# Weight splits off POOL, rope tables queued late, convolution banks copied out raw, and a first stage fed by quarters of x

## The chip, the cores and the metric

The kernel runs on one core of a Trainium2 chip. It holds one program with five engines: TensorE (PE, with PEld for its weight loads), VectorE (DVE), ScalarE (ACT), GpSimd (POOL) and SyncE (SP). PE multiplies into PSUM, DVE and ACT do elementwise work, POOL does a little of it, SP issues most transfers. The time is the device time of one launch in microseconds. Three runs of the kernel before took 995.56, 997.72 and 1001.56 us, the median is 997.72 us.

## The reference

Two decoder layers over 256 tokens of width 1024. Each layer is a half-weighted SwiGLU feed-forward stage (FFN), a mixer, and another FFN; in layer 0 the mixer is a gated short convolution beside cross-attention over 256 memory tokens, in layer 1 it is causal attention on a shared compressed key/value (MLA) beside the same cross-attention. Everything is float32.

```python
def swiglu(h, w13, w2):
    gate, up = jnp.split(h @ w13, 2, axis=-1)
    return (jax.nn.silu(gate) * up) @ w2

def short_conv_mixer(h, w_in, conv_w):
    proj = h @ w_in
    gate_b, gate_c, xt, q_mem = jnp.split(proj, [CONV_CH, 2 * CONV_CH, 3 * CONV_CH], axis=-1)
    return gate_b * causal_short_conv(gate_c * xt, conv_w), q_mem

for layer in range(2):
    x = x + 0.5 * swiglu(rms_norm(x, g[layer, 0]), w13[layer, 0], w2[layer, 0])
    h = rms_norm(x, g[layer, 1])
    ...                                   # mixer: convolution (0) or MLA (1), and memory attention
    x = x + jnp.concatenate([y_mix, y_mem], -1) @ w_out[layer]
    x = x + 0.5 * swiglu(rms_norm(x, g[layer, 2]), w13[layer, 1], w2[layer, 1])
```

D_MODEL is 1024 and D_FF 2816. rms_norm divides each token by the root of its mean square.

## The kernel before, in words

The residual stream `xT` stays in SBUF, channels on partitions, as 8 blocks of 128 channels by 256 tokens. Weights stream from HBM in units of 128 x 1024 (512 KB).

**Splits.** PE multiplies in a reduced-precision float32 mode, so each operand is split into a high part (a rounded cast on ACT) and a low part (raw minus high, a two-input subtraction). A product is then three matmuls (`mm3`), or, where the moving side holds high and low next to each other in 512 columns, a 512-column one and a 256-column one (`mm2`, L193 and L194); below this couple is called a pair. The low part of a weight unit is L87, run on DVE, or on POOL for the units named in `on_pool`: column block 2 of each FFN (two units) and the first w2 unit of each FFN, and three units of the convolution's input weights (`CIN_POOL`).

**Streams.** Class `Stream` A carries w13, the mixers' input weights and the memory weights, B carries w2 and the output weights. Each loads some units ahead (SP issues), casts them (ACT, L86) and subtracts (L87), in the order in which they will be used. A has four raw buffers and six split ones, B two and four.

**An FFN** (`ffn`) has 22 column blocks j. Block j takes two A units (the lower and the upper half of x's channels, c = 0 and 1), 8 pairs each, into two PSUM banks (`pg`, `pm`). ACT copies half a bank out, DVE adds the other half (L434, L435), DVE multiplies by the row factor R (L439), then SiLU (ACT), gate times up (DVE), a split of that product, and 24 matmuls with w2 that accumulate in four banks `acc`.

**The row factor.** The norm's 1/rms per token isn't applied to x. Projections of raw x start at once, and R scales them afterwards. `r_row` makes it: PE sums squares over channels (L289, called r_col below), DVE takes a reciprocal root in a chain of some twelve tiny 128x2 instructions (L165, L153 to L160), DVE builds two diagonal matrices `dg` (L301), PE spreads them (L303), DVE copies R (L306).

**The mixer of layer 0** (`conv_mixer`) takes 20 A units in ten blocks (n = 0 to 9), 24 matmuls a unit, into one bank each; the bank pool `pg` has two banks. Its blocks are read out of PSUM by DVE with R at once (L648), so the first two banks come free only after R, and R's matmul stands ahead of the last quarter of the first two blocks (`pairs`, `late` false).

**The start.** SP issues x in four quarters and the first A units in pieces (unit 0 in four, units 1 to 4 in two), in one queue; the gains of the norm come first. Unit by unit, blocks 0 and 1 are multiplied against the lower half of x, then against the upper half. The rope tables (cosine and sine of positions, about ten small DVE instructions and two on ACT, L704 to L729) stand in the FFN's block 3.

The code is recorded by a tile framework, which orders each engine's queue by its own list scheduling and adds semaphores; an engine then runs its queue strictly in that order.

Of the kernel before, what the change touches and what calls it, by code (L numbers as in the profile page):

```python
# [16 lines left out]
P = 128  # L17
T = 256
# [9 lines left out]
CIN_POOL = ((2, 0), (2, 1), (3, 1))  # L28
# [18 lines left out]
class Stream:  # L47


    def __init__(self, tc, raw_pool, hl_pool, name, units, load_ahead, split_ahead, pieces={}, on_pool=()):  # L50
# [5 lines left out]
        self.pieces, self.on_pool = pieces, on_pool  # L56
        self.hl = {}
        self.hold = ()

    def ahead(self, upto_load, upto_split):  # L60
        nc = self.tc.nc
        while self.loaded < min(upto_load, len(self.units)):
            key, src, n, own = self.units[self.loaded]
            r = self.raw_pool.tile([P, U], F32, name=f"{self.name}raw")
            pieces = self.pieces.get(self.loaded, 1)
            m = n // pieces
            for o in range(0, n, m):
                nc.sync.dma_start(out=r[:, o:o + m], in_=src[:, o:o + m])
            self.raw[self.loaded] = (r, pieces)
            self.loaded += 1  # L70
        while self.splitted < min(upto_split, self.loaded):
            key, src, n, own = self.units[self.splitted]
            r, pieces = self.raw.pop(self.splitted)
            self.split(r, pieces, n, own, nc.gpsimd if key in self.on_pool else nc.vector)
            self.splitted += 1

    def split(self, r, pieces, n, own, eng):
        nc = self.tc.nc
        h = None
        if own is not None:  # L80
            own(r)
        else:
            h = self.hl_pool.tile([P, 2, U], F32R, name=f"{self.name}hl")
            m = n // pieces
            for o in range(0, n, m):
                nc.scalar.copy(out=h[:, 0, o:o + m], in_=r[:, o:o + m])  # L86
                eng.tensor_tensor(out=h[:, 1, o:o + m], in0=r[:, o:o + m], in1=h[:, 0, o:o + m].bitcast(F32),  # L87
                                  op=ALU.subtract)
        self.hl[self.splitted] = h
# [17 lines left out]
def trunk(ctx: ExitStack, tc: tile.TileContext, a, out):  # L107
# [138 lines left out]
    for l in range(2):  # L246
# [144 lines left out]
    def pairs(keyf, row, bank=bank1):  # L391

        st = {}
        late = bank is not bank1

        def go(n):
            if n == 0:
# [8 lines left out]
            if n == 1:  # L406
                if late:
                    proj(keyf(1, 1), st["p1"], 1)
# [11 lines left out]
    def ffn(l, f, inserts, next_norm):  # L420
        go, st = pairs(lambda j, c: ("w13", l, f, j, c), r_row(xs["tot"], abank), lambda: (bank(), mbank()))
        ready = {}
        with tc.issue_after(xs["fed"][0].ins):
            A.ahead(A.used + 6, A.used + 6)
            B.ahead(B.used + 2, B.used + 1)

# [11 lines left out]
        def make(j, e):  # L438
# [8 lines left out]
            act = nc.scalar.activation(out=sl, in_=e[:, 0, :], func=AF.Silu)  # L447
            if j == 0:
# [180 lines left out]
    def conv_mixer(next_norm, pl):  # L629
# [4 lines left out]
        go, st = pairs(lambda j, c: ("cin", j, c), r_row(xs["tot"]))  # L634
# [7 lines left out]
        def project(upto):  # L642
            while st["n"] < upto:
# [3 lines left out]
                e = ev.tile([P, 2, T], F32, name="ev") if n else area[:, 0]  # L647
                evac = nc.vector.tensor_tensor(out=e, in0=ps, in1=rb(st["R"]), op=ALU.mult)  # L648
                if n == 0:
# [432 lines left out]
    for q in (1, 2, 3):  # L1082
        load_x(q)
# [124 lines left out]
```

## Time and profile before

| what | value |
|---|---|
| median of three runs | 997.72 us |
| the profiled execution | 996.72 us, its span 994.9 us |
| mean granted clock of TensorE | 0.995 of full speed |
| PE / DVE / ACT / POOL busy | 98% / 74% / 55% / 7% of the span |
| HBM traffic | 174 GB/s over the span |

The span runs from the first to the last instruction, some 1.8 us lie around it. Busy shares are of the whole span; the stages differ, so the rows further down are taken from single stretches. Times in rows are microseconds from the span's start. In a timeline row the first number is the start, the second the duration; square brackets hold the engine's idle time before it and what ended it. PEclk is the granted clock of TensorE as a share of 2.4 GHz: 0.50 is the lower level, 1.2 GHz.

### The profile page before, as it was taken

Reading aid. Unit: us, or ns where it says so; the run is one execution under the profiler, and the core shown is the slowest. Engines: PE = TensorE matmul, PEld = TensorE weight load, DVE = VectorE, ACT = ScalarE, POOL = GpSimd, SP = SyncE. Lnnn points to the kernel's source line nnn. Section 1 sums busy time; section 2 is a strip of 40 time slices with the busy share of each in tenths; the row PEclk is TensorE's granted clock in tenths of the full one; section 3 lists DMA queues with packets and bytes.
Section 4 is the critical chain, followed back from the end, with each engine's and each line's share of the span. In section 5 each row is a group of like instructions: output and inputs, shape, how many; then the busy total and the mean of one; then the engine's idle time right before and its main releaser. Section 6 shows DMA issues by size and latency. Waiting matters only on the chain.

```text
span 994.9 us, 16997 instructions
## 1 busy us (share of the span) xinstructions
PE 971.8 (98%) x6602; PEld 893.3 (90%) x6602; DVE 734.8 (74%) x1325; ACT 551.0 (55%) x933; POOL 67.6 (7%) x73
## 2 busy tenths in 40 slices
PE   7899999998999999999999999999999999999998
PEld 6789999998989999999999998899997999999997
DVE  6998666676876787666669887766689789666653
ACT  5666545555453655555547555555556776555541
POOL 4120000002001200000011100000011020000000
PEclk9999999999999999999999999999999999999999
DMA  7677656651655286665535765556324428655611
GB/s 265 222 251 241 194 187 190 183 178 64 209 160 171 62 296 210 188 188 186 179 101 180 233 209 185 179 185 188 114 97 127 149 85 312 189 182 186 187 47 43
DMA packets 50192, 174.18 MB, mean 175 GB/s; under 512 B 5824, under 2 KB 6848, under 8 KB 50112
## 3 DMA queue, kind: packets, MB, share of 16 engines
q1 hardware_dynamic: 49968, 172.98, 54.3%
q8 instruction: 51, 0.84, 0.3%
q14 instruction: 29, 0.24, 0.1%
q10 hardware_dynamic: 144, 0.13, 0.0%
HBM read 172.04 MB, written 1.05 MB: 174 GB/s over the span
## 4 chain that ended last, share of the span: by engine, by line
PE 87%; DVE 7%; DMA 2%; ACT 1%; issue 1%; SPq 0%; DVEq 0%; ACTq 0%
PE pm L193 16%; PE pg L193 15%; PE acc L187 10%; PE acc L188 10%; PE acc L189 10%; PE pm L194 8%; PE pg L194 8%; PE pg L187 2%; PE pg L188 2%; PE pg L189 2%; DVE ahl L87 1%; DMA braw<-in_wo 1%; PE pm L187 1%; PE pm L189 1%; PE pm L188 1%
## 5 line engine op out<-in xcount | busy, mean ns | idle before, releaser
L87 DVE TENSOR_TENSOR ahl<-araw,ahl 128x1024 fp32r<-128x1024 f32 (+3 forms) x216 | 254.0, 1180 | 84.8 <-ACT ahl L86 84.4
L86 ACT CAST ahl<-araw 128x1024 fp32r<-128x1024 f32 (+4 forms) x228 | 229.8, 1012 | 128.1 <-PE pm L194 83.0
L193 PE MATMUL pg<-xs,ahl 128*128 128x512 f32 x704 | 258.3, 400 | 3.5 <-DVE xs L183 3.1
L193 PE MATMUL pm<-xs,ahl 128*128 128x512 f32 x704 | 257.5, 400 | 0.7 <-DVE rsy_kn L160 0.7
L188 PE MATMUL acc<-g,bhl 128*128 128x256 f32 x832 | 235.8, 284 | 0.0
L189 PE MATMUL acc<-g,bhl 128*128 128x256 f32 x832 | 235.0, 283 | 0.0
L187 PE MATMUL acc<-g,bhl 128*128 128x256 f32 x832 | 233.7, 284 | 0.6 <-ACT g L179 0.6
L194 PE MATMUL pg<-xs,ahl 128*128 128x256 f32 x704 | 198.6, 282 | 0.1
L194 PE MATMUL pm<-xs,ahl 128*128 128x256 f32 x704 | 197.9, 281 | 0.0
L87 DVE TENSOR_TENSOR bhl<-braw,bhl 128x1024 fp32r<-128x1024 f32 x100 | 122.3, 1224 | 60.1 <-ACT bhl L86 59.7
L193 PEld LDWEIGHTS pg<-xs,ahl 128*128 128x128 f32 x704 | 133.2, 189 | 32.8 <-DVE xs L183 3.8
L193 PEld LDWEIGHTS pm<-xs,ahl 128*128 128x128 f32 x704 | 132.5, 188 | 33.5 <-issue 1.0
L187 PEld LDWEIGHTS acc<-g,bhl 128*128 128x128 f32 x832 | 157.3, 190 | 5.7 <-ACT g L179 1.4
L188 PEld LDWEIGHTS acc<-g,bhl 128*128 128x128 f32 x832 | 158.5, 191 | 0.3 <-DVE g L180 0.2
L189 PEld LDWEIGHTS acc<-g,bhl 128*128 128x128 f32 x832 | 158.6, 191 | 0.1
L86 ACT CAST bhl<-braw 128x1024 fp32r<-128x1024 f32 x104 | 108.7, 1048 | 79.2 <-PE acc L189 53.7
L194 PEld LDWEIGHTS pg<-xs,ahl 128*128 128x128 f32 x704 | 134.0, 190 | 1.3 <-DVE ahl L87 1.3
L194 PEld LDWEIGHTS pm<-xs,ahl 128*128 128x128 f32 x704 | 133.3, 189 | 0.1
L434 ACT COPY sq<-pm 128x256 f32<-128x256 f32 x88 | 32.8, 373 | 69.6 <-PE pm L194 69.3
L439 DVE TENSOR_TENSOR ev<-ev,R 128x512 f32<-128x512 f32 x88 | 61.5, 702 | 2.3
L435 DVE TENSOR_TENSOR ev<-pm,sq 128x256 f32<-128x256 f32 x88 | 37.1, 421 | 32.8 <-ACT sq L434 32.6
L447 ACT ACTIVATE silu<-ev 128x256 f32<-128x256 f32 x88 | 36.6, 417 | 36.7 <-DVE ev L439 36.6
(319 smaller groups left out, 1133.5 us busy)
## 6 DMA issues: line engine op xcount, KB each, us to landing
araw<-in_w SPq DMA_DIRECT2D x171, 512.0 KB, 3.7
braw<-in_w SPq DMA_DIRECT2D x88, 512.0 KB, 4.2
araw<-in_cin SPq DMA_DIRECT2D x20, 512.0 KB, 3.6
braw<-in_wo SPq DMA_DIRECT2D x16, 512.0 KB, 3.8
araw<-in_wmem SPq DMA_DIRECT2D x8, 512.0 KB, 4.3
araw<-in_qin SPq DMA_DIRECT2D x5, 512.0 KB, 3.5
araw<-in_w SPq DMA_DIRECT2D x8, 256.0 KB, 5.5
araw<-in_mem SPq DMA_DIRECT2D x4, 512.0 KB, 4.7
```

The source lines that it names most:

```text
L86: nc.scalar.copy(out=h[:, 0, o:o + m], in_=r[:, o:o + m])
L87: eng.tensor_tensor(out=h[:, 1, o:o + m], in0=r[:, o:o + m], in1=h[:, 0, o:o + m].bitcast(F32), op=ALU.subtract)
L187: nc.tensor.matmul(o, lhs[0], rhs[0], start=start, stop=False, skip_group_check=True)
L188: nc.tensor.matmul(o, lhs[0], rhs[1], start=False, stop=False, skip_group_check=True)
L189: nc.tensor.matmul(o, lhs[1], rhs[0], start=False, stop=stop, skip_group_check=True)
L193: nc.tensor.matmul(o, lhs[0], x, start=start, stop=False, skip_group_check=True)
L194: nc.tensor.matmul(o[:, 0, :], lhs[1], x[:, 0, :], start=False, stop=stop, skip_group_check=True)
L434: nc.scalar.copy(out=part[:, s, :], in_=ps[s][:, 1, :])
L435: nc.vector.tensor_tensor(out=e[:, s, :], in0=ps[s][:, 0, :], in1=part[:, s, :], op=ALU.add)
L439: evac = nc.vector.tensor_tensor(out=e, in0=e, in1=rb(st["R"]), op=ALU.mult)
L447: act = nc.scalar.activation(out=sl, in_=e[:, 0, :], func=AF.Silu)
```

## The change

1. `on_pool` and `pieces` go. Every weight unit's low part is made on DVE.
2. The rope tables move from block 3 to block 15 of the first FFN, and wait for the block before to be evacuated.
3. In `conv_mixer` R is taken after all of blocks 0 and 1. Their two banks are copied out raw by ACT and multiplied by R afterwards in SBUF (`arrived` holds what followed an evacuation before).
4. The first FFN has a head of its own: x in quarters q, and of the first four units the halves that belong to quarter q. After each quarter come 8 pairs: blocks 0 and 1, two channel blocks. The transfers are issued from two queues: SP has all of x, the later units and the rest, ACT has the gains and three pieces of units 0 and 1. The units after that are loaded and split as the quarters pass.

```diff
-    A = Stream(tc, araw, ahl, "a", a_units, 6, 5, {0: 4, 1: 2, 2: 2, 3: 2, 4: 2},
-               {("w13", l, f, 2, c) for l in range(2) for f in range(2) for c in range(2)}
-               | {("cin", j, c) for j, c in CIN_POOL})
-    pool_split = {("w2", l, f, j) for l in range(2) for f in range(2) for j in (0,)}
-    B = Stream(tc, braw, bhl, "b", b_units, 3, 2, {}, pool_split)
+    A = Stream(tc, araw, ahl, "a", a_units, 6, 5)
+    B = Stream(tc, braw, bhl, "b", b_units, 3, 2)
...
+            if n == 0 and head is not None:
+                st["p0"], st["p1"] = bank(), bank()
+                for q in range(4):
+                    head(q)
+                    c = q // 2
+                    for j in range(2):
+                        ps = st[f"p{j}"]
+                        w = heads[2 * c + j]
+                        for k in (2 * q, 2 * q + 1):
+                            for s in range(2):
+                                o = k % 4 * 256 + s * P
+                                mm2(ps[s], (w[:, 0, o:o + P], w[:, 1, o:o + P]), xs["hl"][:, k], k == 0, k == KD - 1)
+                        if q == 3 and j == 0:
+                            next(row)
...
-        go, st = pairs(lambda j, c: ("cin", j, c), r_row(xs["tot"]))
+        go, st = pairs(lambda j, c: ("cin", j, c), r_row(xs["tot"]), late=True)
...
+            if st["n"] == 0:
+                es = [area[:, 0], ev.tile([P, 2, T], F32, name="ev")]
+                for n, e in enumerate(es):
+                    nc.scalar.copy(out=e, in_=go(n))
+                for n, e in enumerate(es):
+                    evac = nc.vector.tensor_tensor(out=e, in0=e, in1=rb(st["R"]), op=ALU.mult)
+                    arrived(n, e, evac)
+                st["n"] = 2
...
+    nc.scalar.dma_start(out=gc[:, 0:8], in_=a["cols"][:, 0:8])
+    load_x(nc.sync, 0)
+    load_w(nc.scalar, 0, 0, 256)
+    load_w(nc.sync, 0, 256, 256)
+    load_w(nc.scalar, 1, 0, 512)
+    load_x(nc.sync, 1)
+    load_w(nc.scalar, 0, 512, 512)
+    load_w(nc.sync, 1, 512, 512)
+    load_x(nc.sync, 2)
+    load_w(nc.sync, 2, 0, 512)
+    load_w(nc.sync, 3, 0, 512)
+    load_x(nc.sync, 3)
+    load_w(nc.sync, 2, 512, 512)
+    load_w(nc.sync, 3, 512, 512)
     nc.sync.dma_start(out=gc[:, 8:], in_=a["cols"][:, 8:])
+    nc.sync.dma_start(out=pos_i, in_=a["pos"])
...
+    def first_head(q):
+        c, o = q // 2, q % 2 * 512
+        feed_split(q, 0)
+        for i in (2 * c, 2 * c + 1):
+            for p in (0, 256) if q == 0 and i == 0 else (0,):
+                n = 256 if q == 0 and i == 0 else 512
+                A.split(raws[i], heads[i], o + p, n)
         feed_square(q, q < 2)
-    A.ahead(5, 4)
-    nc.sync.dma_start(out=pos_i, in_=a["pos"])
+        if q == 2:
+            A.ahead(HEAD + 2, HEAD)
+        if q == 3:
+            B.ahead(1, 0)
+            A.ahead(HEAD + 4, HEAD + 2)
 
     def rope_later():
-        rope_tables(w1)
+        with tc.issue_after(xs["evac"]), tc.issue_after(xs["act"]):
+            rope_tables(w1)
         yield
```

What this does to the queues is shown at three places. First PE in the first stage, where R's matmul (reading `dg`) stands. Banks 232 and 233 are those of column block 1 before, 374 that of block 2; in the changed kernel 368 and 369 are those of block 2. Before:

```order
L194 MATMUL pm_233<-xs_123,ahl_207 128x256
L193 MATMUL pm_233<-xs_123,ahl_207 128x512
L194 MATMUL pm_233<-xs_123,ahl_207 128x256
L193 MATMUL pg_374<-xs_123,ahl_215 128x512
L303 MATMUL acc3_323<-dg_322,ones_108 128x128 x2
L194 MATMUL pg_374<-xs_123,ahl_215 128x256
```

Now (the line of R's matmul is L300):

```order
L194 MATMUL pm_369<-xs_122,ahl_269 128x256
L193 MATMUL pm_369<-xs_122,ahl_269 128x512
L194 MATMUL pm_369<-xs_122,ahl_269 128x256
L193 MATMUL pg_368<-xs_122,ahl_272 128x512
L300 MATMUL acc3_316<-dg_315,ones_108 128x128 x2
L194 MATMUL pg_368<-xs_122,ahl_272 128x256
```

Before, R's matmul follows the 32 pairs of blocks 0 and 1; now it follows those and the 8 pairs of block 2's first unit. Between r_col and R's matmul stand 13.5 pairs before and 12 now.

Then DVE in the first stage, in the middle of the root's chain. Before:

```order
L155 TENSOR_SCALAR rsy_x<-rsy_x 128x2
L704 CAST pos_f<-pos_i 128x2
L158 SCALAR_TENSOR_TENSOR rst_x<-rsy_x 128x2
L707 TENSOR_SCALAR r_ang<-gc,pos_f 128x32
L159 TENSOR_TENSOR rst_x<-rst_x,var_x 128x2
L707 TENSOR_SCALAR r_ang<-gc,pos_f 128x32
L160 SCALAR_TENSOR_TENSOR rsy_x<-rst_x,rsy_x 128x2
L435 TENSOR_TENSOR ev<-pm,sq 128x256
```

Now (L452 is the evacuation that was L435):

```order
L155 TENSOR_SCALAR rsy_x<-rsy_x 128x2
L452 TENSOR_TENSOR ev<-pg,sq 128x256
L158 SCALAR_TENSOR_TENSOR rst_x<-rsy_x 128x2
L452 TENSOR_TENSOR ev<-pm,sq 128x256
L159 TENSOR_TENSOR rst_x<-rst_x,var_x 128x2
L559 TENSOR_TENSOR mem_gqk<-gc 128x1
L844 TENSOR_TENSOR mla_gqk<-gc 128x1
L160 SCALAR_TENSOR_TENSOR rsy_x<-rst_x,rsy_x 128x2
```

The rope tables' instructions have left the chain; the four evacuations of blocks 0 and 1 stand in it.

Last DVE in the convolution, from the middle of the same chain to the first weight splits. Before:

```order
L160 SCALAR_TENSOR_TENSOR rsy_x<-rst_x,rsy_x 128x2
L301 TENSOR_SCALAR dg<-ident,rsy_x 128x128 x2
L306 COPY R<-pm 128x256
L648 TENSOR_TENSOR spare<-pg,R 128x512
L648 TENSOR_TENSOR ev<-pg,R 128x512
L87 TENSOR_TENSOR ahl<-araw,ahl 128x1024 x2
L87 TENSOR_TENSOR bhl<-braw,bhl 128x1024 x2
```

Now (weight splits are L68, and the two multiplications by R, L666, read SBUF):

```order
L160 SCALAR_TENSOR_TENSOR rsy_x<-rst_x,rsy_x 128x2
L68 TENSOR_TENSOR ahl<-araw,ahl 128x1024
L158 SCALAR_TENSOR_TENSOR rst_x<-rsy_x 128x2
L159 TENSOR_TENSOR rst_x<-rst_x,var_x 128x2
L160 SCALAR_TENSOR_TENSOR rsy_x<-rst_x,rsy_x 128x2
L158 SCALAR_TENSOR_TENSOR rst_x<-rsy_x 128x2
L159 TENSOR_TENSOR rst_x<-rst_x,var_x 128x2
L160 SCALAR_TENSOR_TENSOR rsy_x<-rst_x,rsy_x 128x2
L298 TENSOR_SCALAR dg<-ident,rsy_x 128x128 x2
L303 COPY R<-pm 128x256
L666 TENSOR_TENSOR spare<-spare,R 128x512
L666 TENSOR_TENSOR ev<-ev,R 128x512
```

One weight split that POOL made now stands inside the chain, and two more follow it, where before only those of DVE's own units did. At the other three FFN starts one A and one B unit now stand ahead of the chain's first instruction.

## Rows read from the trace of the kernel before

**Rows 1.** What PE waited for, whole span: total us, times, longest us.
```profile
PE acc L303 <- DVE dg L301: 5.8, 1, 5.8
PE pg L193 <- DVE xs L183: 3.1, 2, 2.6
PE pm L303 <- DVE dg L301: 2.7, 1, 2.7
```

**Rows 2.** Busy time of each engine in six stretches.
```profile
core 0: us, PE busy (x) PEld busy (x) DVE busy (x) ACT busy (x) POOL busy (x), PEclk, DMA share, GB/s
12.00:15.40 3.40, 3.35 (x10) 2.34 (x11) 3.40 (x10) 3.40 (x8) 0.40 (x1) 0.50 0.90 327
...
23.63:29.61 5.98, 0.15 (x2) 0.00 (x1) 5.98 (x15) 1.27 (x2) 4.69 (x2) 0.95 0.60 185
29.61:32.50 2.89, 2.89 (x10) 2.65 (x11) 2.46 (x8) 0.70 (x3) 0.00 (x0) 0.50 0.51 177
...
36.88:66.80 29.92, 28.97 (x198) 26.65 (x196) 28.94 (x40) 24.70 (x42) 5.64 (x4) 1.00 0.76 263
...
140.00:160.00 20.00, 20.00 (x139) 18.51 (x138) 13.77 (x21) 10.78 (x17) 0.00 (x0) 1.00 0.60 185
...
247.50:250.90 3.40, 3.40 (x18) 3.40 (x17) 0.42 (x1) 0.63 (x1) 0.00 (x0) 0.50 0.00 0
```

**Rows 3.** Timeline of DVE, first stage, in the root's chain.
```profile
23.74 2.30 DVE L159 TENSOR_TENSOR rst_x<-rst_x,var_x 128x2 f32<-128x2 f32 x1
...
28.67 0.15 DVE L159 TENSOR_TENSOR rst_x<-rst_x,var_x 128x2 f32<-128x2 f32 x1
...
29.27 0.48 DVE L301 TENSOR_SCALAR dg<-ident,rsy_x 128x128 f32<-128x128 f32 x2
```

**Rows 4.** Timeline of POOL, first stage, one of its weight splits.
```profile
23.64 2.38 POOL L87 TENSOR_TENSOR ahl<-araw,ahl 128x1024 fp32r<-128x1024 f32 x1 [0.67 <-ACT ahl L86]
```

**Rows 5.** Timeline of PE: a wait for x, and two pairs in steady work.
```profile
10.44 0.50 PE L193 MATMUL pg<-xs,ahl 128*128 128x512 f32 x1 [2.56 <-DVE xs L183]
...
36.17 0.40 PE L193 MATMUL pm<-xs,ahl 128*128 128x512 f32 x1
...
36.53 0.40 PE L193 MATMUL pm<-xs,ahl 128*128 128x512 f32 x1
```

**Rows 6.** Timeline of ACT and SP's issues, the start.
```profile
0.73 1.28 ACT L131 ACT_TABLE_LOAD   x1 [0.73 <-PEq L1197]
1.18 0.42 SPq L1077 DMA_DIRECT2D xT<-in_x  x1
...
3.55 1.38 SPq L1077 DMA_DIRECT2D xT<-in_x  x3
...
4.38 0.91 ACT L182 ACTIVATE xs<-xT,gc 128x256 fp32r<-128x256 f32 x2 [2.15 <-DMA xT<-in_x]
```

**Rows 7.** Rate of all transfers, 0 to 40 us, a number per microsecond.
```profile
GB/s 0 4 160 249 304 173 86 230 301 386 396 402 395 389 287 41 66 225 414 426 410 422 410 279 172 303 45 221 279 102 348 82 16 0 0 0 0 115 315 164
```

**Rows 8.** Timelines of POOL, DVE and PE at the convolution's start.
```profile
239.64 4.75 POOL L87 TENSOR_TENSOR ahl<-araw,ahl 128x1024 fp32r<-128x1024 f32 x2 [6.16 <-ACT ahl L86]
...
239.75 2.33 DVE L159 TENSOR_TENSOR rst_x<-rst_x,var_x 128x2 f32<-128x2 f32 x1
242.12 2.29 DVE L160 SCALAR_TENSOR_TENSOR rsy_x<-rst_x,rsy_x 128x2 f32<-128x2 f32 x1
244.44 0.16 DVE L158 SCALAR_TENSOR_TENSOR rst_x<-rsy_x 128x2 f32<-128x2 f32 x1
...
246.05 0.68 PE L303 MATMUL pm<-dg,ones 128*128 128x128 f32 x4 [2.72 <-DVE dg L301]
```

**Rows 9.** Groups by line and shape, whole span: count, busy us, mean ns.
```profile
L87 DVE TENSOR_TENSOR ahl<-araw,ahl 128x1024 fp32r<-128x1024 f32 x194 | 236.8, 1224 | 80.3 <-ACT ahl L86 80.1
...
L87 POOL TENSOR_TENSOR ahl<-araw,ahl 128x1024 fp32r<-128x1024 f32 x10 | 24.1, 2418 | 372.1 <-ACT ahl L86 355.5 <-PE pg L189 13.5 <-DVE xs L183 3.1
...
L610 ACT COPY sq<-pm 128x512 f32<-128x512 f32 x8 | 4.3, 582 | 0.1
```

More of the change, by code (lines that the diff above doesn't have):

```diff
@@ L47, with __init__ @@
 class Stream:
[L50 removed]
+    def __init__(self, tc, raw_pool, hl_pool, name, units, load_ahead, split_ahead):
         self.tc, self.raw_pool, self.hl_pool, self.name = tc, raw_pool, hl_pool, name
@@ L55, in __init__, with load_tile, hl_tile, split @@
         self.raw = {}
-        self.pieces, self.on_pool = pieces, on_pool
         self.hl = {}
         self.hold = ()
+    def load_tile(self):
+        return self.raw_pool.tile([P, U], F32, name=f"{self.name}raw")
+    def hl_tile(self):
+        return self.hl_pool.tile([P, 2, U], F32R, name=f"{self.name}hl")
+    def split(self, r, h, o, n):
+        nc = self.tc.nc
+        nc.scalar.copy(out=h[:, 0, o:o + n], in_=r[:, o:o + n])
+        nc.vector.tensor_tensor(out=h[:, 1, o:o + n], in0=r[:, o:o + n], in1=h[:, 0, o:o + n].bitcast(F32),
+                                op=ALU.subtract)
     def ahead(self, upto_load, upto_split):
@@ L63, in ahead @@
             key, src, n, own = self.units[self.loaded]
[L64 to L69, printed above, removed]
+            r = self.load_tile()
+            nc.sync.dma_start(out=r[:, 0:n], in_=src[:, 0:n])
+            self.raw[self.loaded] = r
             self.loaded += 1
@@ L72, in ahead @@
             key, src, n, own = self.units[self.splitted]
-            r, pieces = self.raw.pop(self.splitted)
-            self.split(r, pieces, n, own, nc.gpsimd if key in self.on_pool else nc.vector)
-            self.splitted += 1
[L77 to L89, printed above, removed]
+            r = self.raw.pop(self.splitted)
+            h = None
+            if own is not None:
+                own(r)
+            else:
+                h = self.hl_tile()
+                self.split(r, h, 0, n)
+            self.hl[self.splitted] = h
+            self.splitted += 1
     def get(self, key):
@@ L389, in trunk, with pairs @@
     bank1 = bank
-    def pairs(keyf, row, bank=bank1):
+    def pairs(keyf, row, bank=bank1, late=False, head=None):
         st = {}
-        late = bank is not bank1
         def go(n):
+            if n == 0 and head is not None:
[12 more added lines that the diff above has]
+                            next(row)
+                for c in range(2):
+                    for j in range(2):
+                        A.get(keyf(j, c))
+                return st["p0"]
             if n == 0:
@@ L418, in rb, with ffn @@
         return R.rearrange("p (o t) -> p o t", o=1).broadcast_to([P, 2, T])
-    def ffn(l, f, inserts, next_norm):
-        go, st = pairs(lambda j, c: ("w13", l, f, j, c), r_row(xs["tot"], abank), lambda: (bank(), mbank()))
+    def ffn(l, f, inserts, next_norm, head=None):
+        go, st = pairs(lambda j, c: ("w13", l, f, j, c), r_row(xs["tot"], abank), lambda: (bank(), mbank()),
+                       True, head)
         ready = {}
-        with tc.issue_after(xs["fed"][0].ins):
-            A.ahead(A.used + 6, A.used + 6)
-            B.ahead(B.used + 2, B.used + 1)
+        if head is None:
+            with tc.issue_after(xs["fed"][0].ins):
+                A.ahead(A.used + 6, A.used + 6)
+                B.ahead(B.used + 2, B.used + 1)
         def begin(j):
```

67 lines of the change are left out of this document (32 added, 35 removed).

## The prediction

> **What bounds the kernel now.** I read the page's busy shares first: PE is busy for 98% of the span, so the work of PE sets nearly all of the time and an edit can only win back what PE loses. The list of PE's waits says where that is [rows 1]: 5.8 us before R's matmul in the first FFN, 3.1 us in two waits for x at the start, 2.7 us before R's matmul in the convolution. The reader is to see that the three largest waits all end on DVE and that each but the second is a single event. These three make 11.6 us and the other nine of that list, none above 1.1 us, 7.4: so no change of this kind can give more than some 19 us and what the clock adds.
>
> Then the table of stretches, for the clock [rows 2]. From 12.0 to 15.4, 29.6 to 32.5 and 247.5 to 250.9 us PE runs at PEclk 0.50, the lower of its two levels, each time shortly after it stood idle for more than 2.5 us [rows 1, 2, 5]. Work at half the clock takes twice as long, so these stretches cost half their length: 1.7, 1.45 and 1.7 us.
>
> Last the timelines of DVE and POOL, for why DVE is late. A 128x2 instruction of the root's chain takes 0.15 us, but 2.30 us while POOL runs a weight split that started at 23.64 [rows 3, 4]. In the convolution two of them take 2.33 and 2.29 us beside POOL's two splits, and 0.16 us once these are over [rows 8]. So DVE stands still while POOL subtracts. In the first stage four instructions stretch like that, by 6.5 us together (the row of the longest stands), and the rope tables' instructions lie between the chain's.
>
> **The change, part by part.**
>
> *First stage, start.* The first matmul needs x's first quarter and 256 columns of unit 0. Before, x was issued at 1.18, as the second transfer, and its split began at 4.38 [rows 6]; it now goes first, 0.4 us earlier. But the 256 columns are issued by ACT, and behind the table load of 1.28 us if the queue waits for that [rows 6]. One offsets the other; I leave the first matmul at 5.9 us, where it was. Bounds: 5.4 and 6.5.
>
> *First stage, feeding.* Quarter q needs 0.75 MB. Summing the rate row gives 0.41 MB moved at 4 us, 0.98 at 7, 1.5 at 9, 2.3 at 11 and 3.1 at 13 [rows 7]. In the new issue order the two pieces that complete the first quarter arrive when some 1.2 MB have moved (8.0 us), the second quarter at 1.8 MB (9.8), the third at 2.3 MB (11), the fourth at 3.1 MB (13). A cast and subtraction add about 1 us. A quarter is 8 pairs, and a pair takes 0.36 us, from one pair's start to the next [rows 5], so 2.9 us. PE then runs quarter 1 in two parts up to 10, quarter 2 from 10.8, and the last two without a wait, to 19.4. The wait before quarter 1's second half is again near 2 us, so I charge one stretch at the lower clock, 1.7 us: 21.1. Between the clock staying up and not I take the middle, 20.2. r_col stands 3.5 pairs (1.25 us) ahead of that: 19.0.
>
> A rule of the Trainium skill bears on the second queue. Rows first: by 5 us the single queue had issued x and all of unit 0 (1.5 MB) and 0.72 MB of it had moved [rows 6, 7], so it wasn't the issuing that held it back. The Trainium skill, page "DMA: Bandwidth & Descriptors", section "Issuing engines are not separate DMA queues", says the same against this part of the change: transfers of all engines share the same 16 DMA engines, and a second issuing engine saves only the first one's issue time. By it the second queue gives at most four issues of 0.42 us, 1.7 us; the sum here counts nothing for it.
>
> The same page, section "Rules for kernel authors", asks for 1 MiB or more per transfer, against these small quarters. The trace disagrees for this shape: from 9 to 13 us 256 KB transfers move 386 to 402 GB/s, from 18 to 22 us 512 KB ones 410 to 426 [rows 7]. By the rows the loss is 5% of some 8 us, 0.4 us.
>
> *First stage, R.* The chain's own instructions follow each other by about 0.2 us. Twelve of them make 2.4 us, the two `dg` 0.48 [rows 3]; four evacuations that now stand among them add 1.4 us, and the last two wait for block 1's end, 1.25 us after r_col, and a copy. I get r_col to R's matmul in 4.9 us, so R's matmul at 23.9 instead of 29.6. In these 4.9 us PE has 12 pairs, 4.3 us, so the wait of 5.8 us shrinks to 0.6.
>
> The gain has three terms: R's matmul 5.7 us earlier; 8 pairs that stood behind it now stand ahead of it, 2.9 us; and the lower clock after the idle time, 1.45 us, is not paid there. Sum 10.0 us. Low end: the fourth quarter lands 2 us late and the chain is 1 us longer, and DVE (97% busy from 36.88 to 66.80 [rows 2]) can't keep up with a PE that is ahead of it, 2 us: 5 us. High end: clock up throughout, 11.7 us.
>
> DVE takes three units over there (two of A, one of B), 3 x 1.22 = 3.7 us [rows 9], but loses the 6.5 us of standing and the rope tables' work, so it is ahead of where it was by 2.8 us or more when R comes. What covers its splits is that they run several units ahead of their use; without this cover each would cost PE its 1.22 us.
>
> *Rope tables.* At block 15 they lie in stretches like 140 to 160 us, where DVE is busy 13.8 of 20 us [rows 2]. Some 3 us of small instructions fit into the 6 us that are free: nothing. If they delayed one evacuation by their whole length, 1 to 2 us; nobody needs their result before the shared key stage.
>
> *Convolution.* Removed: the wait of 2.72 us and the lower clock behind it, 1.70 us, 4.4 us together [rows 1, 2, 8]. The chain from r_col without POOL is 4.3 us shorter; one split of 1.22 us now stands in it [rows 9]. On PE, 24 matmuls (2.9 us) move from behind R's matmul to before it. So R is there 5 us or more before PE wants it, and the wait goes for two reasons. Added: two ACT copies of 128x512, about 0.58 us each [rows 9], while ACT has nothing to do; they free the banks before R, so the third block needn't wait. What is late next is DVE: three splits more, 3.7 us, against 4.3 us of standing that is saved. DVE is then only 0.6 us ahead of before, PE 4.4 us. The bounds are 0.6 and 4.4 us. PE has three blocks of work (8.6 us) before it needs a convolved tile, and the tiles' instructions now stand earlier in DVE's queue, so I take a value near the upper end, 3.7.
>
> *The other three FFN starts.* POOL's splits there made DVE stand too, but PE had enough pairs to hide it: none of the rows of waits is theirs [rows 1]. Two splits now stand ahead of the chain, 2.4 us, in place of two stretched instructions of up to 2.3 us. Nothing.
>
> Sum: 10.0 + 3.7 = 13.7 us. The profiled execution took 996.72 us, so 983.0; the median of the three runs lies 1.0 us above that execution. I take half of it: 983.5 us.
>
> **Rivals.**
>
> *The head only moves its wait.* PE waits for x's later quarters and unit 1's pieces as it waited for R: the feeding follows the rate row, in which 6 and 7 us show 86 and 230 GB/s [rows 7], and a second lower-clock stretch follows. For it: nothing in the change makes these early rates higher. Against: by 13 us all is there, and R came at 29.6. Then the low end of the head, 5 us, and 3.7: 988 us.
>
> *DVE takes PE's place.* After R both engines start some 10 us earlier but DVE's queue up to 66.8 us is 97% full [rows 2], and in the convolution DVE gains only 0.6 us. For it: those two numbers. Against: nearly all of the 97% is splits made ahead. Then half of the head and the lower bound of the convolution: 996.7 - 5 - 0.6, so 991 us.
>
> *Slower: DVE's stretched instructions aren't POOL's doing.* If they waited for something else, the waits of 5.8 and 2.7 us would stay, and 15 units more lie on DVE (two of A and one of B in each FFN, three in the convolution). Where DVE sets the pace, in the first 67 us and in the convolution, that is 6 x 1.22 = 7.3 us on the path, against 3 us from the reordering: 1001 us. It decides at a chain instruction that still takes over 1 us with POOL idle. Against it: the three pairs of rows that show the stretch also show POOL's split over the same time [rows 3, 4, 8].
>
> *It doesn't do what it says.* The scheduler puts the head's order so that gains and losses cancel: 996.7 us. The queue's order speaks against it: the rope work has left the chain and R's matmul has moved.
>
> **How the numbers follow.** A difference below 0.5% (5 us) can't be told from none here. Chances: forecast 0.60, its own range 979 to 987; head only moves its wait 0.19; DVE takes PE's place 0.11; no effect 0.06; slower 0.04. The upper end reaches to the second rival's 991 and half a microsecond more for the spread of runs; the lower one is the high end of both terms (11.7 + 4.4 = 16.1, so 980.6) and the 1.7 us that a second queue could save, so 978.5. All but the last two cases are faster by over 5 us, the second only just, so I give faster 0.88, same 0.08, slower 0.04.
>
> **What would show it.** Right: no wait of PE over 1 us at R's matmul in the first FFN and none in the convolution; R's matmul near 24 us; chain instructions at 0.15 to 0.2 us throughout; no stretch with PEclk 0.50 near 30 and near 247 us; PE idle less than 8 us in all. Wrong: PE waits over 2 us on ahl, ev or g between 25 and 70 us (DVE's place), or on g in the convolution; first matmul later than 6.5 us; R's matmul later than 27 us; a lower clock stretch after 25 us.

## The result and the profile after

The changed kernel takes 984.55 us, median of four runs (983.43 to 985.05), the kernel before 997.51 us beside it: a ratio of 0.9863, interval 0.9832 to 0.9895. The forecast was 983.5 us. The profiled execution took 984.37 us after 996.72, with a span of 982.6 after 994.9, so the trace has to account for 12.3 us. The total was forecast well, but its two terms were each about 3 us off, to opposite sides.

The page's busy rows first. PE has the same 6602 matmuls and DVE is no busier, though it does all the splits; POOL's 67.6 us have become 31.1.

```profile
span 982.6 us, 16958 instructions
PE 969.2 (99%) x6602; PEld 891.0 (91%) x6602; DVE 724.4 (74%) x1339; ACT 551.8 (56%) x933; POOL 31.1 (3%) x57
```

What PE waited for (total us, times, longest us), to set beside [rows 1]. Neither wait for R is in it any more. At its head is a new one, of 1.9 us, which also ends on DVE.

```profile
PE pm L187 <- DVE ev L452: 1.9, 1, 1.9
PE pg L194 <- DVE ahl L68: 1.4, 3, 0.7
PE pm L1133 <- POOL ones L135: 1.1, 1, 1.1
PE pg L187 <- ACT spare L881: 1.1, 1, 1.1
```

The same stages by time, clock and traffic (columns as in [rows 2]). The two stretches that ran at PEclk 0.50 behind the start's waits and behind R, and the one in the convolution, are at 1.00. One new stretch is at 0.51, from 59.62 to 62.98 us, just behind the new wait; it costs half its length, 1.7 us.

```profile
core 0: us, PE busy (x) PEld busy (x) DVE busy (x) ACT busy (x) POOL busy (x), PEclk, DMA share, GB/s
12.00:15.40 3.40, 3.40 (x21) 2.97 (x20) 3.40 (x9) 3.40 (x8) 0.00 (x0) 1.00 0.75 295
29.61:32.50 2.89, 2.89 (x21) 2.61 (x20) 2.89 (x3) 1.85 (x4) 0.00 (x0) 1.00 0.71 217
...
59.62:62.98 3.36, 3.36 (x18) 3.36 (x17) 3.36 (x7) 2.76 (x5) 0.00 (x0) 0.51 0.93 322
...
247.50:250.90 3.40, 3.40 (x31) 3.40 (x30) 3.40 (x7) 1.60 (x3) 0.00 (x0) 1.00 0.89 310
```

Where the 12.3 us arise is read from matmuls that both kernels have at the same place of the work. The four small matmuls of a root's row sum are such a mark: in the memory part of the first FFN, at the convolution, at the second FFN and at the last. Timeline of PE, the kernel before, then the changed one:

```profile
65.35 0.50 PE L289 MATMUL pm<-ones,mem_tot 128*128 128x1 f32 x4
...
238.41 0.50 PE L289 MATMUL pm<-ones,tot 128*128 128x1 f32 x4
...
334.73 0.50 PE L289 MATMUL acc<-ones,tot 128*128 128x1 f32 x4
...
806.77 0.50 PE L289 MATMUL acc<-ones,tot 128*128 128x1 f32 x4
```

```profile
55.87 0.50 PE L286 MATMUL pm<-ones,mem_tot 128*128 128x1 f32 x4
...
231.54 0.50 PE L286 MATMUL pm<-ones,tot 128*128 128x1 f32 x4
...
321.19 0.50 PE L286 MATMUL acc<-ones,tot 128*128 128x1 f32 x4
...
794.46 0.50 PE L286 MATMUL acc<-ones,tot 128*128 128x1 f32 x4
```

The reader subtracts: the changed kernel is ahead by 9.5 us at the memory's root, by 6.9 at the convolution's, by 13.5 at the second FFN's and by 12.3 at the last one's, and 12.3 at the end. So 9.5 were won at the head, 2.6 given back around the memory key, 6.7 won in the convolution, and 1.2 given back later.

What was given back at 58 us shows in the queues of DVE, POOL, SP and ACT, and in PE's next matmul. PE's matmuls for the memory key need the bank that the block's evacuation (L452) frees. On DVE that stands behind two splits, together 2.35 us.

```profile
49.57 2.80 DVE L183 SCALAR_TENSOR_TENSOR spare<-araw,gc,spare 128x256 fp32r<-128x256 f32 x3
...
55.23 2.35 DVE L68 TENSOR_TENSOR ahl<-araw,ahl 128x1024 fp32r<-128x1024 f32 x2
57.51 0.42 DVE L452 TENSOR_TENSOR ev<-pg,sq 128x256 f32<-128x256 f32 x1
57.85 0.41 DVE L452 TENSOR_TENSOR ev<-pm,sq 128x256 f32<-128x256 f32 x1
...
49.25 1.55 POOL L502 TENSOR_TENSOR mem_sum<-mem_sum,sq 128x512 f32<-128x512 f32 x1 [0.49 <-ACT sq L501]
50.88 0.81 POOL L505 TENSOR_TENSOR mem_tot<-mem_sum 128x256 f32<-128x256 f32 x1
...
52.43 0.33 SPq L76 DMA_DIRECT2D araw<-in_w  x1
...
56.16 1.04 ACT L67 CAST ahl<-araw 128x1024 fp32r<-128x1024 f32 x1 [1.89 <-DMA araw<-in_w]
57.11 0.36 ACT L451 COPY sq<-pg 128x256 f32<-128x256 f32 x1
...
58.32 0.39 PE L187 MATMUL pm<-ahl,spare 128*128 128x256 f32 x1 [1.95 <-DVE ev L452]
```

The two splits alone don't make it late. The evacuation also needs ACT's copy (L451), which ends at 57.47 us, just when DVE comes free; without the splits it could hardly have begun earlier. ACT's copy stands behind a cast that waited 1.89 us for its load. SP issued that load at 52.43 us, right after the last of the three L183 had ended. These split the memory's own tokens, out of the same raw buffers; beside two of the sums that POOL still makes for the memory they took 2.80 us, where four of them at 43.54 took 1.67. So DVE is late twice, once directly and once through the buffer that it frees late. That the load waited for just that buffer is read from the times, not tested.

Before, the same place cost two waits of 0.97 and 0.68 us; now it costs 1.95, 0.68 and the 1.7 us of the lower clock. The difference is 2.7 us, against 2.6 from the marks.

### The profile page after: what moved, and what is told of

Read it like the earlier page. It is cut to its first block, busy times and chain, and to the rows that moved or that the text cites. A ratio compares the mean times of both kernels' runs of the same rounds, so it can differ in the third digit from the quotient of the medians.

```text
span 982.6 us, 16958 instructions
## 1 busy us (share of the span) xinstructions
PE 969.2 (99%) x6602; PEld 891.0 (91%) x6602; DVE 724.4 (74%) x1339; ACT 551.8 (56%) x933; POOL 31.1 (3%) x57
## 3 DMA queue, kind: packets, MB, share of 16 engines
HBM read 172.04 MB, written 1.05 MB: 176 GB/s over the span
## 4 chain that ended last, share of the span: by engine, by line
PE 82%; DVE 10%; DMA 5%; ACT 2%; issue 1%; DVEq 0%; SPq 0%; ACTq 0%
PE pm L193 15%; PE pg L193 14%; PE acc L189 9%; PE acc L187 9%; PE acc L188 9%; PE pm L194 8%; PE pg L194 7%; DVE ahl L68 4%; PE pg L187 2%; DVE bhl L68 2%; PE pg L188 2%; PE pg L189 2%; DMA araw<-in_w 2%; DMA braw<-in_wo 2%; DVE spare L183 1%
## 5 line engine op out<-in xcount | busy, mean ns | idle before, releaser
L68 DVE TENSOR_TENSOR ahl<-araw,ahl 128x1024 fp32r<-128x1024 f32 (+3 forms) x226 | 268.8, 1196 | 82.5 <-ACT ahl L67 82.2
L67 ACT CAST ahl<-araw 128x1024 fp32r<-128x1024 f32 (+3 forms) x226 | 229.6, 1019 | 132.5 <-PE pm L194 86.8
L194 PE MATMUL pg<-xs,ahl 128*128 128x256 f32 x704 | 198.2, 282 | 1.4 <-DVE ahl L68 1.4
L68 DVE TENSOR_TENSOR bhl<-braw,bhl 128x1024 fp32r<-128x1024 f32 x104 | 126.9, 1222 | 62.5 <-ACT bhl L67 62.4
L451 ACT COPY sq<-pm 128x256 f32<-128x256 f32 x88 | 32.7, 372 | 68.7 <-PE pm L194 68.5
L452 DVE TENSOR_TENSOR ev<-pm,sq 128x256 f32<-128x256 f32 x88 | 37.1, 422 | 35.0 <-ACT sq L451 35.0
L187 PE MATMUL pg<-xs,ahl 128*128 128x256 f32 x192 | 55.2, 288 | 0.0
```

Source lines behind the costliest of these rows:

```text
L67: nc.scalar.copy(out=h[:, 0, o:o + n], in_=r[:, o:o + n])
L68: nc.vector.tensor_tensor(out=h[:, 1, o:o + n], in0=r[:, o:o + n], in1=h[:, 0, o:o + n].bitcast(F32), op=ALU.subtract)
L187: nc.tensor.matmul(o, lhs[0], rhs[0], start=start, stop=False, skip_group_check=True)
L194: nc.tensor.matmul(o[:, 0, :], lhs[1], x[:, 0, :], start=False, stop=stop, skip_group_check=True)
L451: nc.scalar.copy(out=part[:, s, :], in_=ps[s][:, 1, :])
L452: nc.vector.tensor_tensor(out=e[:, s, :], in0=ps[s][:, 0, :], in1=part[:, s, :], op=ALU.add)
```

## The experiments

All ratios are to the kernel before on the same chip. Twelve kernels ran, four on each of three chips; the kernel before took 996.26 us beside e1 to e4, 996.46 beside e5 to e8 and 996.39 beside e9 to e12. e9 ran once, for its profile, and is not in the table. The table gives the median, the ratio with its interval, when R's matmul of the first FFN started, and two lengths from the marks: from the start to the convolution's mark (A), and from there to the second FFN's (B).

```
                            us      ratio  interval        R      A       B
before                      -       1                      29.61  238.41  96.32
changed                     984.55  0.9863 0.9832-0.9895   23.62  231.54  89.65
e1  splits off POOL only    988.55  0.9917 0.9902-0.9932   27.38  233.12  90.86
e2  splits back on POOL     988.92  0.9922 0.9902-0.9942   25.83  237.52  89.50
e3  old head                986.63  0.9901 0.9883-0.9919   27.55  234.17  89.48
e4  banks not copied        987.06  0.9898 0.9881-0.9915   23.74  233.27  90.52
e5  changed, again          986.05  0.9895 0.9867-0.9923   23.80  233.32  89.55
e6  one queue               987.72  0.9911 0.9884-0.9938   25.57  232.43  89.51
e7  rope tables early       986.13  0.9890 0.9864-0.9916   24.12  231.58  89.57
e8  memory later            982.22  0.9858 0.9832-0.9885   23.82  230.45  89.43
e10 e8, memory sums on DVE  982.53  0.9856 0.9834-0.9879   23.73  227.80  89.30
e11 e10, no sums on POOL    982.41  0.9851 0.9829-0.9873   24.55  228.81  89.47
e12 e8, again               984.64  0.9881 0.9861-0.9902   23.78  228.65  89.51
```

The changed kernel and e8, each timed twice, moved by 1.5 and 2.4 us from one time to the next. So medians closer than that are not told apart here; the marks of one execution tell more, but those in A still vary by 1.8 us between two executions of the same kernel.

A holds the clock too. One stretch at the lower clock lasts 3.4 us and costs 1.7. Up to the convolution's mark the kernel before, e2 and e3 have two of them, the changed kernel, e1, e4, e5 and e8 one, e6, e7, e10, e11 and e12 none.

**e1, the splits alone.** The kernel before with

```
-            self.split(r, pieces, n, own, nc.gpsimd if key in self.on_pool else nc.vector)
+            self.split(r, pieces, n, own, nc.vector)
```

> The kernel before, with its ten POOL weight splits put on DVE and nothing else changed. Theory (POOL's splits hold DVE's small instructions up): the root's chain runs at 0.15 to 0.2 us each in the first FFN and in the convolution, R's wait of 5.8 us falls under 2 us, that of 2.7 us in the convolution goes, with the lower clock behind both: 986 to 990 us, 988. Rival (rope work and the queue's order make the chain late, POOL's splits cost nothing): the wait of 5.8 us stays near 5 and the added splits lie on DVE: 995 to 999 us.

988.55 us, as the theory had it. (The edit moves all fifteen units of `on_pool`; the ten of the expectation are only the full A units.) The chain's instruction that took 2.30 us [rows 3] takes 0.16 (first row), although the rope's still stand among the chain's, and R's wait of 5.8 us is the second row, of the list of waits:

```profile
26.54 0.16 DVE L159 TENSOR_TENSOR rst_x<-rst_x,var_x 128x2 f32<-128x2 f32 x1
...
PE acc L303 <- DVE dg L301: 0.4, 1, 0.4
```

The convolution's wait for R is gone as well. So this one edit gives 8.3 us by the ratio (6.8 to 9.8).

In the first stage it does so in two ways, for the scheduler also changed PE's queue: between r_col and R's matmul stand 47 matmuls (23.5 pairs) instead of 27. R's matmul is only 2.2 us earlier (27.38 after 29.61), since three splits now lie on DVE in the chain; the other 3.6 us of the wait are covered by the ten pairs that moved ahead of it. In the convolution 36 matmuls stand there in both kernels, so there the wait goes by the faster chain alone.

**e2, the splits back on POOL.** The changed kernel with

```
-        nc.vector.tensor_tensor(out=h[:, 1, o:o + n], in0=r[:, o:o + n], ...
+        eng = nc.gpsimd if key in self.on_pool else nc.vector
+        eng.tensor_tensor(out=h[:, 1, o:o + n], in0=r[:, o:o + n], ...
```

> The changed kernel with the ten weight splits back on POOL. Theory: chain instructions in the first FFN and the convolution take over 1 us again; R comes about 4 us later in the first FFN, PE waits 2 to 4 us there and runs at the lower clock after it, and 1 us or less in the convolution, where the copied banks cover 2.9 us: 986 to 991 us, 988. Rival (POOL's splits do no harm, the order of the head gave the gain): DVE is relieved of ten splits, the wait of 1.95 us before the memory key goes: 981 to 984 us.

The time came as expected, the place not quite. The scheduler put the root's chain behind POOL's first two splits, and what stood still was what lay beside them: three 128x1 products (0.15 us elsewhere) and the split of a gate tile, 2.59 us for 0.41. Timeline of POOL, then of DVE:

```profile
16.44 5.80 POOL L69 TENSOR_TENSOR ahl<-araw,ahl 128x1024 fp32r<-128x1024 f32 x2 [5.99 <-ACT ahl L68]
29.80 3.36 POOL L69 TENSOR_TENSOR bhl<-braw,bhl 128x1024 fp32r<-128x1024 f32 x1 [7.56 <-ACT bhl L68]
```

```profile
17.25 2.41 DVE L563 TENSOR_TENSOR mem_gqk<-gc 128x1 f32<-128x1 f32 x2
...
19.92 2.34 DVE L848 TENSOR_TENSOR mla_gqk<-gc 128x1 f32<-128x1 f32 x1
...
30.86 2.59 DVE L181 TENSOR_TENSOR g<-gg,g 128x256 fp32r<-128x256 f32 x1
```

R's matmul waits 0.56 us, not 2 to 4; more is paid at the row sum (1.2) and at the gate tile (1.8), and behind the latter the clock falls to 0.50 from 35.08 to 38.49 us. The wait of 2.3 us at the memory key's second half, with another fall behind it, can't be laid to the splits: e5 below, which has none on POOL, waits 2.6 us there. At the convolution's mark e2 is 6.0 us behind the changed kernel, or 4.2 behind e5. In the convolution POOL's splits cost nothing once the banks are copied: B is 89.50.

**e3, the old head.** The changed kernel with

```
-    ffn(0, 0, {...}, 1, first_head)
+    A.ahead(1, 0); feed_split(0, 0); ...      # loads and splits as before, all on SP
+    ffn(0, 0, {...}, 1)
```

> The changed kernel with the first stage's old loading and order of matmuls (one queue, whole units, x in quarters behind unit 0), the other three parts of the change kept. Theory (the head's own part is the start's waits and the 2.9 us of pairs that now stand before R, the rest of the gain is POOL's and the rope tables'): waits for x of 3.1 us at the start with the lower clock after it, R's wait under 2 us: 987 to 990 us, 988.5. Rival (the loading by quarters is what brings R early): R's wait stays over 4 us, 992 to 995 us. Second rival (DVE takes PE's place after the head anyway): a head that is 3 us later lets the wait before the memory key shrink, 984 to 986 us.

986.63 us, between the theory's range and the second rival's. Waits for x of 2.2 us are there, R's is not. At the memory's mark it is 3.4 us behind the changed kernel (59.31 after 55.87), at the convolution's 2.6, or 0.9 if e5's trace is taken for it. The old loading brings back the lower clock at the start (0.50 from 13.97 to 17.38 us), 1.7 us of this. So the head's loading is worth 1 to 3 us, and part of it is lost again before the convolution.

**e4, banks not copied.** The changed kernel with

```
-        go, st = pairs(..., late=True)
+        go, st = pairs(...)
...
-                    nc.scalar.copy(out=e, in_=go(n))
...
+                    evac = nc.vector.tensor_tensor(out=e, in0=ps, in1=rb(st["R"]), op=ALU.mult)
```

> The changed kernel with the convolution's first two banks scaled straight from PSUM and R's matmul at its old place (no raw copies by ACT). Theory (the chain without POOL's splits is in time by itself): R's matmul waits under 1 us, the third block perhaps 1 us for a bank: 984 to 986.5 us. Rival (the raw copies remove the wait): the wait of 2.7 us and the lower clock come back, 988 to 990 us.

R's matmul waits for nothing here either. B is 90.52, 0.9 above the changed kernel's; one wait of 1.3 us for a tile of ACT's is in it. Together with e1 and e2: against the convolution's 96.32 us, the splits alone give 5.5 to 5.8, the copies alone 6.8, both 6.7. The two cures overlap almost wholly. The 2.5 us by which e4's median lies above the first one of the changed kernel arise mostly ahead of the convolution (1.7 in A), where the edit changes nothing.

**e5 and e6, one queue.** e5 is the changed kernel again; e6 has

```
-    nc.scalar.dma_start(out=gc[:, 0:8], ...)
-    load_w(nc.scalar, 0, 0, 256)               # and two more
+    nc.sync.dma_start(out=gc[:, 0:8], ...)
+    load_w(nc.sync, 0, 0, 256)                 # and two more
```

> The changed kernel unaltered, as the base on the same chip for the other kernels of this call: 984.5 us, 983 to 986, by every theory. Its wait before the memory key's matmuls is expected at 1 to 2.5 us again, since nothing of its cause changes from run to run.

> The changed kernel with the four loads of the start that ACT issued put on SP's queue, at the same places in the order. Theory (the engines' rate bounds the start, not the issuing): every piece within 1 us of where it was, first matmul at 6 to 6.8 us, the total the same within 1 us. Rival (the second queue is what feeds the quarters): up to four issues of 0.42 us later and a longer wait before the first quarter's second half, with the lower clock: 2 to 3.5 us slower.

e5 gave 986.05 us, just past the range expected; its wait before the memory key is 2.0 us, and one of 2.6 us follows at the key's second half, where the changed kernel's first profile has 0.68. These 1.9 us are the difference of the two executions in A.

In e6 the rival was right on the head. The pieces do come later with one queue, and PE waits longer for the second quarter's split:

```profile
12.51 0.39 PE L194 MATMUL pg<-xs,ahl 128*128 128x256 f32 x1 [1.76 <-DVE ahl L68]
```

R's matmul is 1.8 us later and the memory's mark 1.9 us later than in e5 (57.63 after 55.71). At the convolution's mark e6 is 0.9 us ahead: 232.43 after 233.32. But e5 has a stretch at the lower clock behind its wait of 2.6 us (0.50 from 78.03 to 81.44), and e6 has none. Without these 1.7 us e6 is 0.8 us behind. The rest of the 1.9 us went into shorter waits at the memory key, 1.6 and 1.7 us for 2.0 and 2.6. Why only e5's clock fell isn't shown, and the medians (1.7 us apart, overlapping intervals) don't settle what the second queue is worth.

**e7, rope tables early.** The changed kernel with the tables at block 3 and without the holds:

```
-        with tc.issue_after(xs["evac"]), tc.issue_after(xs["act"]):
-            rope_tables(w1)
+        rope_tables(w1)
...
-    inserts(rope_later(), 15)
+    inserts(rope_later(), 3)
```

> The changed kernel with the rope tables' instructions back where the scheduler had them, among the chain's (13 of them). Theory (they cost their own 0.15 to 0.2 us each, 2 to 2.5 us, on a chain that has no slack): R comes 1 to 2 us later, PE waits under 1.5 us for it, total 0 to 2 us slower than the base. Rival (they are nothing, since each chain instruction waits for the one before it and the rope's fit between): R within 0.5 us of 23.6, same total.

R at 24.12, 0.3 us later; same total. The rival was right: the rope's instructions run in the chain's own gaps.

**e8 and e12, the memory later.** The changed kernel with

```
-**inserts(mem_kv(0), 6, 7), **inserts(mem_kv(1), 10, 11)
+**inserts(mem_kv(0), 8, 9), **inserts(mem_kv(1), 11, 12)
```

and the units moved likewise.

> The changed kernel with the two memory inserts of the first FFN at blocks 8, 9 and 11, 12 in place of 6, 7 and 10, 11, and their units moved with them in the load order. Theory (DVE is full up to 66 us because it builds its lead of splits, so the memory's eight splits come too early for it): the wait of 1.95 us before the memory key's matmuls and the lower clock behind it go, 2.5 to 3.5 us faster than the base. Rival (the memory's matmuls take a PSUM bank of the running block, wherever they stand): the same wait two blocks later, same total within 1 us.

> The kernel of e8 once more, as the base of e10 and e11 on the same chip: 982.2 us, 981 to 984.5, by every theory.

982.22 and 984.64 us, the second just past its range. The wait at the key's second half (2.6 us in e5) is gone, the one at L452 has moved along: 2.0 us in e8, 1.0 in e12. Behind it the clock falls in e8 (0.50 from 75.27 to 78.68 us) and not in e12, which makes their difference of 1.8 us in A. So each side has half of it.

**e9, kinds of POOL work.** The changed kernel with six POOL instructions on a tile of their own beside each chain (memset, copy, product, difference).

> The changed kernel with a POOL instruction of another kind beside each root's chain, on a tile that nothing else uses: six each of a memset in the first FFN, a copy in the convolution and in the attention, a multiplication by a constant in the second FFN, a subtraction of two tiles in the third and fourth. Each starts when the chain's first value is there. Theory (DVE waits for POOL where both read SBUF and the DVE instruction has two SBUF inputs; the Trainium skill, SBUF - State Buffer, Who interferes with whom, says so): the memset stretches nothing, the copy, the multiplication and the subtraction stretch the chain's TENSOR_TENSOR and SCALAR_TENSOR_TENSOR from 0.16 us to about the length of one POOL instruction, 0.2 us and more, and leave its TENSOR_SCALAR at 0.16 us. Rival (only long subtractions of two tiles do it): the copy and the multiplication stretch nothing. One look, no time is drawn from it.

Timeline of POOL, then of DVE an instruction of the chain with two tile inputs beside each kind (beside the last three kinds the longest of that stage):

```profile
21.54 2.05 POOL L305 MEMSET scr<- 128x224 f32 x6
...
235.18 3.54 POOL L307 COPY scr<-scr 128x224 f32<-128x224 f32 x6
...
326.01 5.05 POOL L309 TENSOR_SCALAR scr<-scr 128x224 f32<-128x224 f32 x6
...
514.27 3.77 POOL L311 TENSOR_TENSOR scr<-scr 128x224 f32<-128x224 f32 x6
```

```profile
23.19 0.15 DVE L160 TENSOR_TENSOR rst_x<-rst_x,var_x 128x2 f32<-128x2 f32 x1
...
237.07 0.32 DVE L159 SCALAR_TENSOR_TENSOR rst_x<-rsy_x 128x2 f32<-128x2 f32 x1
...
326.11 0.28 DVE L159 SCALAR_TENSOR_TENSOR rst_x<-rsy_x 128x2 f32<-128x2 f32 x1
...
514.38 0.47 DVE L159 SCALAR_TENSOR_TENSOR rst_x<-rsy_x 128x2 f32<-128x2 f32 x1
```

The memset stretches none of them, the copy and the product stretch some of them to 0.22 to 0.37 us, the difference to 0.38 to 0.47. That is less than one of these POOL instructions (0.6 to 0.8 us), but the rival, that only subtractions do it, is out. The Trainium skill, page "SBUF — State Buffer", section "Who interferes with whom", names a port pair that VectorE and GpSimd share and that one instruction holds to its end; a VectorE instruction with two SBUF inputs contends only with a GpSimd instruction that reads SBUF. The trace agrees with that for these four kinds.

**e10 and e11, sums off POOL.** e8 with

```
-                nc.gpsimd.tensor_tensor(out=mem_st["sum"], in0=mem_st["sum"], in1=sq, op=ALU.add)
+                nc.vector.tensor_tensor(out=mem_st["sum"], in0=mem_st["sum"], in1=sq, op=ALU.add)
```

(e10, and the last sum likewise); e11 also takes the head's squares and sums off POOL.

> The kernel with the memory inserts at blocks 8, 9 and 11, 12, and in addition the three additions and the last one of the memory's squares on DVE in place of POOL. Theory (POOL's additions hold DVE's two-input instructions up like the splits did: 1.78 us for 0.68, 1.76 for 1.22, 1.98 for 1.22): DVE pays 3 x 0.69 + 0.42 = 2.5 us of its own and loses some 4 us of standing, the wait of 2.0 us before the memory key falls under 1.2 us, 1 to 3 us faster than e8. Rival (the wait is for the PSUM bank of the block that has just ended, which no faster DVE can shorten): same time within 1 us.

> As e10, and in addition the first stage's squares of quarters 0 and 1 on ACT and their sums on DVE, so that POOL does nothing while the quarters are split. Theory: the splits of 128x256 in the first quarter, which take 3.29 us for three, run in about 0.4 us each, the waits of 1.4 us in all before the second halves of the quarters fall under 0.6 us: 0.5 to 1.5 us faster than e10. Rival (ACT and DVE, now with the squares and 1.1 us of sums, bring the chain as much later as the splits come earlier): same within 0.7 us, R later than 24.5 us.

In e12 POOL's sums still hold DVE up (first fence); in e10 instructions of the same shapes run in their own time (second).

```profile
66.08 1.98 DVE L68 TENSOR_TENSOR bhl<-braw,bhl 128x1024 fp32r<-128x1024 f32 x1
67.99 1.78 DVE L456 TENSOR_TENSOR ev<-ev,R 128x512 f32<-128x512 f32 x1
```

```profile
65.62 0.68 DVE L456 TENSOR_TENSOR ev<-ev,R 128x512 f32<-128x512 f32 x1
66.22 1.22 DVE L68 TENSOR_TENSOR ahl<-araw,ahl 128x1024 fp32r<-128x1024 f32 x1
```

The wait at L452 falls to 0.5 us in e10 and is not in e11's list. The medians are 2.1 and 2.2 us under e12's, with overlapping intervals: likely, not settled, and e10 lies 0.3 above e8's first. In e11 R comes later, as its rival said, and nothing is won on e10. e10, e11 and e8's first median (ratios 0.9851 to 0.9858) are the lowest here, some 2 to 4 us under the changed kernel's two; they are not told apart from each other.

## Why the prediction was right, and where it was not

**POOL's splits were the main cause.** Taking them off the old kernel gives 8.3 us (e1), putting them back into the new one stretches DVE's small instructions again and costs 4 to 6 us up to the convolution (e2), and e9 shows it by kind. The rival that they weren't is out. What isn't separated is how much of the first stage's gain came from the chain and how much from the order that the scheduler then gave PE.

**The head's times held.** Row sum 19.0 forecast, 18.84 measured; R's matmul 23.9 and 23.62. The first matmul was forecast at 5.9 and came at 6.29. ACT's queue didn't wait for the table load (it issued at 1.24 us); what came late were the gains, which ACT now issues: x's split waited for them until 5.00 us. With one queue (e6) it starts at 4.34 and the first matmul comes at 5.87. The lower clock charged there was not paid: the wait of near 2 us came as three of 0.44, 0.73 and 0.20 us, and the clock stayed up. The wait of 0.6 us for R didn't come.

**The head's gain was kept in part only.** The failed step is the sentence on DVE, "What covers its splits is that they run several units ahead of their use": by it the sum put DVE's part at nothing and banked all of PE's lead. The lead of "2.8 us or more" that it gave DVE was about right: the fifth split of stream B starts at 56.10 us before and at 53.76 now, 2.3 earlier. But PE was 9.5 us ahead there. Of these, 2.6 were lost at the memory key, where the bank came free late, behind DVE's splits and behind a load that waited for DVE. That is the rival "DVE takes PE's place", in part; the low end of the range priced it at 2 us. e6 agrees: with PE 1.9 us later, the waits are 1.2 us shorter. The term of 10.0 measured 6.9.

**The convolution was mis-sized.** 3.7 was forecast with an upper bound of 4.4; it gave 6.7. The bound held R's wait and the clock behind it, and left out two waits further on: 1.12 us at 271.15 before a transpose, which ends on DVE, and 0.61 at 288.02 for a cast of ACT's. Neither is in the changed kernel. The first is gone in e1 too, so it followed from DVE's lateness; the second stays in e1 (0.62 us) and goes in e2, which points to the copied banks. Some 0.5 us of the 6.7 are not accounted for. "DVE is then only 0.6 us ahead" was too careful: behind R its next splits start 2.2 us further ahead than PE's lead of 6.9 alone would make them (stream B's first at 244.97 after 254.01). And R is there 3.2 us before PE wants it (the chain ends at 235.95, R's matmul starts at 239.18), not "5 us or more"; the prediction's own terms, 4.3 - 1.2 + 2.9 - 2.7, give 3.3.

**The other FFN starts: not settled.** 1.2 us went between the second FFN's mark and the last one's (473.27 after 472.04; 472.21 in e2, with the splits on POOL). But with the splits on DVE this length is 472.24 in e8 and 473.47 in e12, which are the same kernel, and 472.06 in e9. So 1.2 us is no more than executions differ by, and the "nothing" of the prediction stands untouched. A part of it shows just ahead of the last FFN: a load of the attention's output weights is issued behind four loads of the other stream, where it stood behind three, and PE waits 0.41 us for its split. SP's issues before, then after, then PE:

```profile
784.08 4.37 SPq L68 DMA_DIRECT2D araw<-in_w  x3
789.29 0.33 SPq L68 DMA_DIRECT2D braw<-in_wo  x1
```

```profile
770.71 5.50 SPq L76 DMA_DIRECT2D araw<-in_w  x4
777.39 0.33 SPq L76 DMA_DIRECT2D braw<-in_wo  x1
...
784.97 0.39 PE L189 MATMUL acc<-g,bhl 128*128 128x256 f32 x1 [0.41 <-DVE bhl L68]
```

Less the lead of 13.5 us that the second FFN's marks show, that load is issued 1.6 us later than before. In e8 the loads go in the same order and PE doesn't wait there. So the order can't be the whole cause; it wasn't tried by itself.

**Rope tables and second queue.** Nothing for either in the sum: e7 agrees. The second queue does give 1.8 us at R (e6), about the four issues of 0.42 us [rows 6]; at the convolution 0.8 us of it is left, if the clock's fall in e5 is taken off.

**The signs.** R's matmul near 24 us, the chain at 0.15 to 0.16 us and PE's waits at R came as "right" had it. Two signs went the other way: PE's waits add up to 9.3 us, not under 8 (19.0 before), and a lower clock stretch did come after 25 us, at the memory key. The lowest bound has a slip: 980.6 less 1.7 is 978.9, not 978.5.

The sum was 10.0 + 3.7 = 13.7, the measurement 6.9 + 6.7 - 1.2 = 12.3. It came so near by luck: two errors of 3 us cancelled, and the 1.2 us lie within what executions differ by.

## What to carry to other kernels

In this kernel work given to POOL wasn't free for DVE: look for tiny DVE instructions that take as long as a POOL instruction beside them. A stage in which the helping engine is full may keep only part of what is won ahead of it, as here, so price the next wait there before adding the gain up. And the upper bound of removing a wait is not that wait alone, where others further on come from the same lateness.

## What was not expected

DVE's one-input instructions aren't all safe from POOL: the chain's `dg` pair, TENSOR_SCALAR with one tile input, took 0.89 us beside POOL's products in e9 and 0.67 beside its differences, 0.48 elsewhere. e9's expectation had left them at their own length. The kernel before shows it too: beside POOL's first split a CAST and a TENSOR_SCALAR of the rope (L704, L707) took 1.27 and 1.23 us, in e1 0.16 and 0.23.

And a wait of about 2 us doesn't always bring the lower clock: after 1.95 us in the changed kernel's first profile it fell to 0.51, after 2.0 us at the same place in e5 it stayed at 1.00, to fall behind the wait of 2.6 us at 77 us. In e11 it fell at 754 us, where PE's two waits just before are of 1.05 and 0.62 us. One such fall is 1.7 us, the whole difference of e8 and e12 in A, but not that of the changed kernel and e5, which have one each.
